# Mixture-of-experts trunk on one core: where the small transposes stand among the expert matrices

## Chip, core and metric

The kernel runs on one core of one Trainium2 chip. The metric is the device time of one execution in microseconds (us), as the median of several runs; lower is better. Everything is float32 at the interface.

## What is computed

One layer of an encoder: attention, a residual layer norm, then a mixture of 32 experts of which each of 1024 tokens takes four, then a second residual layer norm. The change touches the experts only. Cut to that part, the reference is:

```python
def clamped_swiglu(h):
    h_glu = jnp.minimum(h[..., 0::2], SWIGLU_LIMIT)
    h_lin = jnp.clip(h[..., 1::2], -SWIGLU_LIMIT, SWIGLU_LIMIT)
    return h_glu * jax.nn.sigmoid(SWIGLU_ALPHA * h_glu) * (h_lin + 1.0)

def expert_block(args):                 # for each block of rows of one expert
    xblk, e = args
    h = xblk @ w_gate_up[e] + b_gate_up[e]           # 1024 -> 2048
    return clamped_swiglu(h) @ w_down[e] + b_down[e]  # 1024 -> 1024
```

The rows of an expert are gathered by a table, and its results are added back into the token rows with the gate as weight.

## The kernel before

**The expert loop.** The loop `for e in range(NE)` runs over 32 experts in an order that a ranking by load sets. In pass `e` it issues `gate_up(e)`, the gathers of the rows of expert `e + 2` (`gather_x`, `gather_o`), and `down(e - 1)`: the down matrix of one expert is multiplied after the gate and up matrix of the next. An expert's weights come in 1 MB tiles of 128 x 2048 floats: eight for gate and up (k = 0 to 7, called g0 to g7 here; tensors `w10g`, `w11g`, ...), four for down (c = 0 to 3, called d0 to d3; `w10d`, ...). The text writes E11 for the pass e = 11, and so on.

**Three products.** For precision every weight tile is split into a high part `wh` (a cast on ACT, line 607) and a low part `wl` (a subtraction on DVE, line 612), and so are the activations (`xTh`, `xTl`, `aTh`, `aTl`). `mm3` (line 57) issues three matmuls of 128 x 512 for each product; in the trace they read wh with the high activation, wh with the low one, then wl with the high one. So a tile is 4 x 3 = 12 matmuls, and its third is the first that needs `wl`. `wh` and `wl` have three buffers each, and `prep(ci + 3)` splits a tile two ahead of the one that PE multiplies: the cast of a tile can start when PE has finished the tile three before it.

**Two row blocks.** Each expert has 128 main rows. Those for which `ovf(e)` holds have also 32 overflow rows (E1 to E8, then the even ones to E28; 18 in all), computed as four quarters side by side: `go` (32 matmuls after g3 and again after g7 in the trace's count) and `yq` after d3.

**Transposes.** Activations must be transposed by PE into PSUM and copied out. `turn` (line 1133) does one batch: up to four 128 x 128 transposes into the PSUM tile `tp`, of which there is one only (tag `tp`, one buffer), then either `split` (a cast on ACT, line 63, and a subtraction on DVE, line 64) for the main rows, or one ACT copy (line 1138) for the overflow rows. In pass e > 1 there are up to six batches: a(e-1) part 0 and part 1 (the activations of the expert before, four transposes each), ao(e-1) (its overflow activations, two), x(e+1) part 0 and part 1 (the rows of the next expert, four each), xo(e+1) (its overflow rows, two). The dictionaries `between` and `between_d` say after which weight tile each goes: a after g0 and g2, ao after g4, x after g6 and after d0, xo after d2.

**What sets the order.** From E2 on PE's order is the order in which the code is written (`manual_schedule` for PE). The orders on DVE, ACT and POOL come from a scheduler that follows the code where it can. Each engine runs its own instructions in that order.

**The activation function.** `swiglu(...).whole()` runs after g7: on DVE two minima of 128 x 512 from PSUM into `act` (line 1179), two clamps into `lin` (line 1183) and one product over 1024 columns (line 1185); on ACT one Silu between them (line 1180).

**A list on the side.** `list_blocks()` in E1 computes, spread over DVE, a small table that is written to DRAM and read back by two DMAs on ACT's queue: `bt` (line 1117) and `blk` (line 1119), which waits for the first to have landed. They come up in E2.

Of the kernel before, what the change touches and what calls it, by code (L numbers as in the profile page):

```python
# [9 lines left out]
F32 = mybir.dt.float32  # L10
# [10 lines left out]
P = 128  # L21
# [3 lines left out]
KD = D // P  # L25
# [3 lines left out]
NE = 32  # L29
# [16 lines left out]
def trunk_kernel(ctx: ExitStack, tc: tile.TileContext, x, w_qkv, q_norm, k_norm, w_o,  # L46
                 lnm_g, lnm_b, lnf_g, lnf_b, r_w, r_b, w_gu, b_gu, w_dn, b_dn,
                 rope_c, rope_s, out):
    nc = tc.nc
# [12 lines left out]
    def split(hi, lo, src):  # L62
        nc.scalar.copy(hi, src)  # L63
        nc.vector.tensor_tensor(lo, src, hi.bitcast(F32), ALU.subtract)  # L64
# [15 lines left out]
    ident = cp.tile([P, P], F32, name="ident")  # L80
# [93 lines left out]
    with tc.tile_pool(name="p1", bufs=1, side="right", reuse_waits="tile") as p1, \  # L174
# [14 lines left out]
        def load_x(i):  # L189
            xts[i] = p_xq.tile([P, D], F32, tag="rows", name=f"xt{i}")  # L190
            nc.sync.dma_start(xts[i], x[i * P:(i + 1) * P, :])

        def turn_x(i):
            xt = xts[i]
            xT = p_xq.tile([P, 2 * KD, P], F32R, tag="cols", bufs=2, name=f"xT{i}")
            hi, lo = xT[:, 0:KD, :], xT[:, KD:, :]
            for h in range(2):
                tp = ps1.tile([P, 4, P], F32, tag="tp", name=f"tp{i}_{h}")
                for c in range(4):
                    k = 4 * h + c  # L200
                    nc.tensor.transpose(tp[:, c, :], xt[:, k * P:(k + 1) * P], ident)
                split(hi[:, 4 * h:4 * h + 4, :], lo[:, 4 * h:4 * h + 4, :], tp)
            xTs[i] = (hi, lo)
            if i + 1 < NT:
                load_x(i + 1)
            else:
                load_q(0)
# [113 lines left out]
        for i in range(NT):  # L321
# [5 lines left out]
            if 1 < i < NT - 1:  # L327
                turn_x(i + 1)
# [708 lines left out]
    with tc.tile_pool(name="moex", bufs=1, side="right", reuse_waits="tile") as mx, \  # L1037
# [5 lines left out]
        xo, xoT, act, actT, acto, actoT = {}, {}, {}, {}, {}, {}  # L1043
# [77 lines left out]
        def ovf(e):  # L1121
            return 1 <= RANK[e] <= NO
# [10 lines left out]
        def turn(src, hi, lo, nk, nm):  # L1133
            tp = ps_t.tile([P, 4, P], F32, tag="tp", name=f"tp{nm}")
            for c in range(nk):
                nc.tensor.transpose(tp[:, c, :], src[:, c * P:(c + 1) * P], ident)  # L1136
            if lo is None:
                nc.scalar.copy(hi, tp[:, 0:nk, :])
            else:
                split(hi, lo, tp[:, 0:nk, :])  # L1140

        def turn_x(e, part):
            if part == 0:
                xT[e] = [mx.tile([P, KD, P], F32R, tag=f"xT{a}", bufs=2, name=f"xT{a}_{e}") for a in "hl"]
                if ovf(e):
                    xoT[e] = mp.tile([P, 2, P], F32, tag="xoT", bufs=2, name=f"xoT{e}")
            if part == 2 and not ovf(e):
                return
            if part < 2:
                turn(xg[e][:, part * 512:(part + 1) * 512], xT[e][0][:, 4 * part:4 * part + 4, :],  # L1150
                     xT[e][1][:, 4 * part:4 * part + 4, :], 4, f"x{e}_{part}")
            else:
                turn(xo[e], xoT[e], None, 2, f"xo{e}")

        def turn_a(e, part):
            if part == 0:

                tag, bufs = ("xT", 2) if e == NE - 1 else ("aT", 1)
                actT[e] = [mx.tile([P, KD, P], F32R, tag=tag + a, bufs=bufs, name=f"aT{a}_{e}") for a in "hl"]
                if ovf(e):  # L1160
                    actoT[e] = mp.tile([P, 2, P], F32, tag="aoT", bufs=1, name=f"aoT{e}")
            if part == 2 and not ovf(e):
                return
            if part < 2:
                turn(act[e][:, part * 512:(part + 1) * 512], actT[e][0][:, 4 * part:4 * part + 4, :],
                     actT[e][1][:, 4 * part:4 * part + 4, :], 4, f"a{e}_{part}")
            else:
                turn(acto[e], actoT[e], None, 2, f"ao{e}")

        def swiglu(ps, w, nm):  # L1170
            n = len(ps)
# [90 lines left out]
        def down(e, between={}):  # L1262
            y = ys.pop(e, None) or mp.tile([P, D], F32, tag="y", bufs=2, name=f"y{e}")
            yp = ps_g.tile([P, D], F32, tag="gu0", name=f"yp{e}") if e == NE - 1 else \
                ps_y.tile([P, D], F32, tag="y", name=f"yp{e}")
            if ovf(e):
                yq = ps_o.tile([P, 512], F32, tag="o", name=f"yq{e}")
            ah, al = actT[e]
            later = []
            for c in range(KD // 2):  # L1270
                fetch(ci[0] + len(order))
                prep(ci[0] + 3)
                hi, lo, w = wts.pop((e, "d", c))
                for j in range(2):
                    k = 2 * c + j
                    for n in range(2):
                        sl = slice(j * D + n * 512, j * D + (n + 1) * 512)
                        mm3(yp[:, n * 512:(n + 1) * 512], ah[:, k, :], al[:, k, :], hi[:, sl], lo[:, sl],
                            k == 0, k == KD - 1)
                later.append((c, w))  # L1280
                if c == KD // 2 - 1:
                    for cc, w in later if ovf(e) else ():
                        ts = slice(cc * OVF, (cc + 1) * OVF)
                        for j in range(2):
                            for n in range(2):
                                sl = slice(j * D + n * 512, j * D + (n + 1) * 512)
                                m = 2 * j + n
                                mm(yq[m * OVF:(m + 1) * OVF], actoT[e][:, j, ts], w[:, sl],
                                   cc == 0, cc == KD // 2 - 1)
                    later.clear()  # L1290
                ci[0] += 1
                if c in between:
                    between[c]()
            nc.scalar.mul(y, yp, gm_s[:, e:e + 1])  # L1294
            nc.gpsimd.indirect_dma_start(  # L1295
                out=fd, out_offset=bass.IndirectOffsetOnAxis(ap=mi[:, e:e + 1], axis=0),
                in_=y, in_offset=None, bounds_check=T + P - 1, oob_is_err=True, compute_op=ALU.add)
            if e == NE - 1:

                idle = ps_y.tile([P, D], F32, tag="y", name="idle")  # L1300
                for r in range(22):
                    mm(idle[:, 0:512], ah[:, KD - 1, :], hi[:, 0:512])
            if not ovf(e):
                return
            H2 = 2 * OVF
            ya = mp.tile([H2, 512], F32, tag="ya", bufs=1, name=f"ya{e}")
            nc.scalar.mul(ya, yq[H2:P], go_s[H2:P, e:e + 1])
            yo = mp.tile([H2, 512], F32, tag="yo", bufs=2, name=f"yo{e}")
            nc.vector.scalar_tensor_tensor(yo, yq[0:H2], go_s[0:H2, e:e + 1], ya, ALU.mult, ALU.add)
            nc.gpsimd.indirect_dma_start(  # L1310
                out=fd2, out_offset=bass.IndirectOffsetOnAxis(ap=toh[:, e:e + 1], axis=0),
                in_=yo, in_offset=None, bounds_check=2 * (T + P) - 1, oob_is_err=True, compute_op=ALU.add)
# [2 lines left out]
        in_turn = ExitStack()  # L1315
        for e in range(NE):
            between = {}
            between_d = {}
            if e > 0:
                for k, part in zip((0, 2, 4) if e > 1 else range(3), range(3)):  # L1320
                    between[k] = lambda part=part: turn_a(e - 1, part)
            if e + 1 < NE:
                if e == 0:
                    between[X1] = lambda: [turn_x(1, part) for part in range(3)]
                else:
                    for k, part in zip((6, 8, 10) if e > 1 else (3, 4, 5), range(3)):
                        (between if k < KD else between_d)[k % KD] = lambda part=part: turn_x(e + 1, part)
            if e == 0:
                with tc.manual_schedule(engines={mybir.EngineType.DVE}):
                    slots(lambda: prep_lo(2))  # L1330
            gate_up(e, between)
            if e == 1:
                list_blocks()

                in_turn.enter_context(tc.manual_schedule(engines={mybir.EngineType.PE}))
            if e + 2 < NE:
                gather_x(e + 2)
                gather_o(e + 2)
            if e == NE - 1:
                between = {1 + part: lambda part=part: turn_a(NE - 1, part) for part in range(3)}  # L1340
                down(e - 1, between)
            elif e > 0:
                down(e - 1, between_d)
        down(NE - 1)
        in_turn.close()

# [7 lines left out]
    for i in range(NT // 2):  # L1354
        f = slot(order[(len(seq) + 1 + i) % len(order)], f"fs{i}")
# [154 lines left out]
```

## Time and profile before

| | |
|---|---|
| median of 3 runs | 2076.91 us (2074.36 to 2081.57) |
| profiled execution | 2077.01 us, span of the trace 2075.2 us |
| mean granted TensorE clock | 0.991 of full speed |
| PE matmul busy | 2005.0 us (97% of the span) |
| DVE busy | 1599.3 us (77%) |
| ACT busy | 1272.2 us (61%) |
| POOL busy | 540.5 us (26%) |
| DMA | 500.44 MB, mean 241 GB/s |

PE is TensorE's matmuls, PEld its weight loads, which overlap them, DVE is VectorE, ACT is ScalarE, POOL is GpSimd. The end of a matmul is modelled in the trace, so rows are best compared by their starts. A number in brackets at the end of a row is the time for which the engine sat idle before it, with the instruction or engine that released it. "xN" means that N like instructions in a row are shown as one. A cast or split whose input is named `w10d` belongs to the down matrix of expert 10, which is multiplied in pass E11.

### The profile page before, as it was taken

The page shows a single profiled execution, that of the slowest core. Times are in us where ns is not written, and L with a number is a line of the kernel's source. Part 1 is how long each engine was busy: PE and PEld are TensorE (multiplying, and loading weights), DVE is VectorE, ACT ScalarE, POOL GpSimd, SP SyncE. Part 2 cuts the span into 40 slices and gives each one's busy share as a digit, 9 for nine tenths or more (in the row PEclk, how much of TensorE's full clock was granted, in tenths as well). Part 3 has the DMA queues.
Part 4 walks back from the last instruction along what each step waited for, and adds up shares of the span by engine and source line. Part 5 has one row for each costly group of instructions (what it writes and reads, how often), then busy time and mean ns, then how long its engine had stood idle before and what let it go on. Part 6 is the DMA issues. An engine that isn't in the chain of part 4 may idle for free. (4 is left out here: it accounts for less than half of the span.)

```text
span 2075.2 us, 28727 instructions
## 1 busy us (share of the span) xinstructions
PE 2005.0 (97%) x10691; PEld 1425.7 (69%) x10691; DVE 1599.3 (77%) x1649; ACT 1272.2 (61%) x1566; POOL 540.5 (26%) x373
## 2 busy tenths in 40 slices
PE   8998999999997999999999999999999999999997
PEld 6775666665675666666676777767777677677774
DVE  6647778776888787777777877878878787787894
ACT  5655555655554566566566766767667666666674
POOL 0215777776134202212211111011111110111100
PEclk9999999999998999999999999999999999999999
DMA  5216000000645687887788888979889889788875
GB/s 174 72 62 178 31 32 21 30 22 17 226 145 213 257 311 277 304 293 295 279 331 296 355 333 311 374 286 341 338 303 357 319 309 371 283 352 326 335 306 183
DMA packets 106353, 500.44 MB, mean 241 GB/s; under 512 B 16001, under 2 KB 17026, under 8 KB 73442
## 3 DMA queue, kind: packets, MB, share of 16 engines
q1 hardware_dynamic: 87360, 447.02, 55.9%
q0 software_dynamic: 16000, 50.90, 8.7%
q8 instruction: 85, 1.39, 0.3%
q10 hardware_dynamic: 2850, 0.66, 0.2%
q14 instruction: 58, 0.48, 0.1%
HBM read 457.05 MB, written 41.49 MB: 240 GB/s over the span
## 5 line engine op out<-in xcount | busy, mean ns | idle before, releaser
L55 PE MATMUL gu<-wh,xTh 128*128 128x512 f32 x1024 | 419.2, 410 | 1.0 <-ACT xTh L63 1.0
L55 PE MATMUL gu<-wl,xTh 128*128 128x512 f32 x1024 | 401.8, 393 | 0.3 <-DVE wl L612 0.3
L55 PE MATMUL gu<-wh,xTl 128*128 128x512 f32 x1024 | 401.1, 392 | 0.0
L448 POOL TENSOR_TENSOR acc<-acc,pt 128x512 f32<-128x512 f32 x152 | 211.8, 1393 | 79.7 <-ACT pt L444 70.1
L55 PEld LDWEIGHTS gu<-wh,xTh 128*128 128x128 f32 x1024 | 193.1, 189 | 54.7 <-issue 14.2
L55 PEld LDWEIGHTS gu<-wl,xTh 128*128 128x128 f32 x1024 | 192.9, 188 | 43.4 <-DVE wl L612 0.7
L55 PEld LDWEIGHTS gu<-wh,xTl 128*128 128x128 f32 x1024 | 193.7, 189 | 36.9 <-DVE xTl L64 0.2
L55 PE MATMUL yp<-wl,aTh 128*128 128x512 f32 x512 | 201.7, 394 | 9.0 <-DVE wl L612 9.0
L55 PE MATMUL yp<-wh,aTh 128*128 128x512 f32 x512 | 206.0, 402 | 0.0
L598 POOL DMA_INDIRECT xg<-xd,mi x32 | 45.9, 1436 | 609.0 <-PE tpx L1136 599.7
L55 PE MATMUL yp<-wh,aTl 128*128 128x512 f32 x512 | 200.0, 391 | 0.0
L434 DVE TENSOR_REDUCE nm<-sc 128x1 fp32r<-128x1024 f32 x124 | 150.6, 1221 | 51.3 <-PE sc L55 50.4
L444 ACT ACTIVATE pt<-st 128x512 f32<-128x512 f32 x256 | 149.4, 596 | 55.5 <-PE st L55 45.9
L1295 POOL DMA_INDIRECT fd<-y,mi x32 | 78.9, 2467 | 302.4 <-ACT y L1294 302.4
L55 PE MATMUL qkv<-wh,xT 128*128 128x512 f32 x384 | 124.3, 404 | 2.6 <-ACT xT L63 1.4
L55 PEld LDWEIGHTS yp<-wl,aTh 128*128 128x128 f32 x512 | 96.1, 188 | 36.5 <-DVE wl L612 15.3
L55 PE MATMUL po<-pt,vn 128*64 128x256 f32 x1024 | 118.5, 384 | 0.0
L55 PEld LDWEIGHTS yp<-wh,aTh 128*128 128x128 f32 x512 | 96.2, 188 | 31.5 <-issue 14.3
L55 PE MATMUL st<-qs,kT_hi 128*128 128x512 f32 x256 | 112.2, 438 | 3.6 <-ACT pt L444 3.0
L55 PEld LDWEIGHTS yp<-wh,aTl 128*128 128x128 f32 x512 | 96.4, 188 | 18.3
L55 PE MATMUL st<-q,kT_lo 128*128 128x512 f32 x256 | 101.9, 398 | 1.3 <-DVE q L148 1.3
L55 PE MATMUL sc<-kT_hi,qs 128*128 128x512 f32 x256 | 101.4, 401 | 1.0 <-DVE nm L434 0.8
(520 smaller groups left out, 4163.9 us busy)
## 6 DMA issues: line engine op xcount, KB each, us to landing
w0g<-in_expert_w_gate_up SPq DMA_DIRECT2D x8, 1024.0 KB
w1g<-in_expert_w_gate_up SPq DMA_DIRECT2D x8, 1024.0 KB
w2g<-in_expert_w_gate_up SPq DMA_DIRECT2D x8, 1024.0 KB
w3g<-in_expert_w_gate_up SPq DMA_DIRECT2D x8, 1024.0 KB
w4g<-in_expert_w_gate_up SPq DMA_DIRECT2D x8, 1024.0 KB
w5g<-in_expert_w_gate_up SPq DMA_DIRECT2D x8, 1024.0 KB
w6g<-in_expert_w_gate_up SPq DMA_DIRECT2D x8, 1024.0 KB
w7g<-in_expert_w_gate_up SPq DMA_DIRECT2D x8, 1024.0 KB
```

Of the source, the lines that this page charges most:

```text
L55: nc.tensor.matmul(o, lhsT=lhsT, rhs=rhs, start=start, stop=stop)
L434: nc.vector.tensor_reduce(nms[n][:, m:m + 1], sc.pop((n, m)), AX.X, ALU.max, negate=True)
L444: nc.scalar.activation(pts[n, k], st, AF.Exp)
L448: (nc.vector if n == NG - 1 or n == NG - 2 and k > 3 else nc.gpsimd).tensor_tensor(accs[n], pts[n, 0] if k == 1 else accs[n], pts[n, k], A ...
L598: return nc.gpsimd.indirect_dma_start(out=xg[e], out_offset=None, in_=xd, in_offset=bass.IndirectOffsetOnAxis(ap=mi[:, e:e + 1] if rows is ...
L1295: nc.gpsimd.indirect_dma_start(out=fd, out_offset=bass.IndirectOffsetOnAxis(ap=mi[:, e:e + 1], axis=0), in_=y, in_offset=None, bounds_chec ...
```

## The change

From E2 on the batches are placed anew, and the two short ones become one. A new function `turn_o(e)` transposes xo(e+1) into columns 2 and 3 of one `tp` tile and ao(e-1) into columns 0 and 1, and issues two ACT copies from it; it stands after g4. x(e+1) part 0 moves from after g6 to after g5, and part 1 from after d0 to after g7. No batch is left in `down(e - 1)` (except in the last pass, which is as before). a(e-1) stays after g0 and g2. Passes E0 and E1 stay as they were.

```diff
+        def turn_o(e):
+
+            tp = ps_t.tile([P, 4, P], F32, tag="tp", name=f"tpo{e}")
+            if e + 1 < NE and ovf(e + 1):
+                for c in range(2):
+                    nc.tensor.transpose(tp[:, 2 + c, :], xo[e + 1][:, c * P:(c + 1) * P], ident)
+                xoT[e + 1] = mp.tile([P, 2, P], F32, tag="xoT", bufs=2, name=f"xoT{e + 1}")
+                nc.scalar.copy(xoT[e + 1], tp[:, 2:4, :])
+            if ovf(e - 1):
+                for c in range(2):
+                    nc.tensor.transpose(tp[:, c, :], acto[e - 1][:, c * P:(c + 1) * P], ident)
+                nc.scalar.copy(actoT[e - 1], tp[:, 0:2, :])
...
-            between_d = {}
-            if e > 0:
-                for k, part in zip((0, 2, 4) if e > 1 else range(3), range(3)):
-                    between[k] = lambda part=part: turn_a(e - 1, part)
+            if e == 1:
+                for part in range(3):
+                    between[part] = lambda part=part: turn_a(e - 1, part)
+            elif e > 1:
+                between[0] = lambda: turn_a(e - 1, 0)
+                between[2] = lambda: turn_a(e - 1, 1)
+                between[4] = lambda: turn_o(e)
...
-                    for k, part in zip((6, 8, 10) if e > 1 else (3, 4, 5), range(3)):
-                        (between if k < KD else between_d)[k % KD] = lambda part=part: turn_x(e + 1, part)
+                    for k, part in zip((5, 7) if e > 1 else (3, 4, 5), range(3)):
+                        between[k] = lambda part=part: turn_x(e + 1, part)
...
-                down(e - 1, between_d)
+                down(e - 1)
```

What this makes of DVE's order, from the split of d0 to that of d3 in pass E11 (`wl136` to `wl139` are d0 to d3 of expert 10, `xTl_12` the low parts of x(12), `act11` and `lin11` the activation function of expert 11). Before:

```order
L612 TENSOR_TENSOR wl136_10267<-w10d0_10094,wh136_10265 128x2048 [waits DMAHW1_49,PE_49,Activation_49]
L612 TENSOR_TENSOR wl137_10295<-w10d1_10124,wh137_10293 128x2048 [waits DMAHW2_49,PE_49,Activation_49]
L64 TENSOR_TENSOR xTl_12_10282<-tpx12_0_10284,xTh_12_10281 128x512 [waits Activation_49]
L1179 TENSOR_SCALAR act11_10122<-gu11_0_10116 128x512 [waits PE_49]
L1179 TENSOR_SCALAR act11_10122<-gu11_1_10117 128x512 [waits PE_49]
L1183 TENSOR_SCALAR lin11_10123<-gu11_0_10116 128x512
L1183 TENSOR_SCALAR lin11_10123<-gu11_1_10117 128x512
L612 TENSOR_TENSOR wl138_10326<-w10d2_10152,wh138_10324 128x2048 [waits DMAHW3_49,Activation_49]
L1185 SCALAR_TENSOR_TENSOR act11_10122<-lin11_10123,act11_10122 128x1024 [waits DVE_49,Activation_49]
L64 TENSOR_TENSOR xTl_12_10282<-tpx12_1_10340,xTh_12_10281 128x512 [waits Activation_49]
L612 TENSOR_TENSOR wl139_10351<-w10d3_10170,wh139_10349 128x2048 [waits DMAHW4_49]
```

The same stretch on DVE with the change:

```order
L612 TENSOR_TENSOR wl136_10274<-w10d0_10088,wh136_10272 128x2048 [waits DMAHW1_49,PE_49,Activation_49]
L64 TENSOR_TENSOR xTl_12_10262<-tpx12_0_10263,xTh_12_10261 128x512 [waits Activation_49]
L1192 TENSOR_SCALAR act11_10116<-gu11_0_10110 128x512 [waits PE_49]
L612 TENSOR_TENSOR wl137_10292<-w10d1_10118,wh137_10290 128x2048 [waits DMAHW2_49,Activation_49]
L1192 TENSOR_SCALAR act11_10116<-gu11_1_10111 128x512 [waits PE_49]
L64 TENSOR_TENSOR xTl_12_10262<-tpx12_1_10306,xTh_12_10261 128x512 [waits Activation_49]
L1196 TENSOR_SCALAR lin11_10117<-gu11_0_10110 128x512
L1196 TENSOR_SCALAR lin11_10117<-gu11_1_10111 128x512
L612 TENSOR_TENSOR wl138_10330<-w10d2_10146,wh138_10328 128x2048 [waits DMAHW3_49,DVE_49]
L1198 SCALAR_TENSOR_TENSOR act11_10116<-lin11_10117,act11_10116 128x1024 [waits DVE_49,Activation_49]
L612 TENSOR_TENSOR wl139_10348<-w10d3_10164,wh139_10346 128x2048 [waits DMAHW4_49,PE_49,Activation_49]
```

The same eleven instructions stand between the two ends. The first minimum and the first `xTl` now come ahead of the split of d1, and the second `xTl` ahead of the clamps.

ACT's order in pass E2 around the two DMAs of the block list (`wh27` is g7 of expert 2, `wh28` d0 of expert 1). Before:

```order
L1117 DMA bt_85<-ebi_6847 128x2 [waits DVE_49]
L607 CAST wh27_7091<-w2g7_6899 128x2048 [waits DMAHW2_49,PE_49,Activation_49]
L1119 DMA blk_4797<-bt_85 1x256 [waits DMAHW7_49]
L1138 COPY aoT1_6968<-tpao1_7085 128x256 [waits PE_49]
L607 CAST wh28_7109<-w1d0_6917 128x2048 [waits DMAHW3_49,PE_49,Activation_49]
L607 CAST wh29_7137<-w1d1_6948 128x2048 [waits DMAHW4_49,PE_49,Activation_49]
L63 CAST xTh_3_7125<-tpx3_0_7128 128x512 [waits PE_49]
```

ACT's order there with the change:

```order
L1117 DMA bt_85<-ebi_6847 128x2 [waits DVE_49]
L607 CAST wh27_7095<-w2g7_6899 128x2048 [waits DMAHW2_49,PE_49,Activation_49]
L1119 DMA blk_4797<-bt_85 1x256 [waits DMAHW7_49]
L1177 COPY xoT3_7088<-tpo2_7085 128x256 [waits PE_49]
L1181 COPY aoT1_6968<-tpo2_7085 128x256 [waits PE_49]
L607 CAST wh28_7122<-w1d0_6917 128x2048 [waits DMAHW3_49,PE_49,Activation_49]
L63 CAST xTh_3_7111<-tpx3_0_7113 128x512 [waits PE_49]
```

The `blk` DMA still stands ahead of the copy that frees `tp`; a second copy stands behind it, and the cast of x(3) part 0 has moved ahead of one weight cast.

## Rows read from the trace of the kernel before

**Rows 1.** Page, busy us, share and instructions of each engine.

```profile
PE 2005.0 (97%) x10691; PEld 1425.7 (69%) x10691; DVE 1599.3 (77%) x1649; ACT 1272.2 (61%) x1566; POOL 540.5 (26%) x373
```

**Rows 2.** Waits of PE, 900 to 2040 us: releaser, total us, times, longest.

```profile
PE yp L55 <- DVE wl L612: 9.0, 13, 0.9
```

**Rows 3.** Timeline of PE: start, us, instruction, idle before; E11, then E30.

```profile
1184.33 0.38 PE L1136 MATMUL tpxo<-ident,xo 128*128 128x128 f32 x2
...
1184.78 0.40 PE L55 MATMUL yp<-wh,aTl 128*128 128x512 f32 x1
1185.85 0.50 PE L55 MATMUL yp<-wl,aTh 128*128 128x512 f32 x1 [0.68 <-DVE wl L612]
1186.19 0.40 PE L55 MATMUL yp<-wh,aTh 128*128 128x512 f32 x1
...
1981.41 0.50 PE L55 MATMUL yp<-wl,aTh 128*128 128x512 f32 x1 [0.92 <-DVE wl L612]
```

**Rows 4.** Timelines of ACT and DVE in E11, from the tile g5 on.

```profile
1166.74 1.91 ACT L607 CAST wh<-w11g 128x2048 fp32r<-128x2048 f32 x1 [0.80 <-PE gu L55]
1168.55 0.37 ACT L1138 COPY aoT<-tpao 128x256 f32<-128x256 f32 x1
1169.72 1.91 ACT L607 CAST wh<-w10d 128x2048 fp32r<-128x2048 f32 x1 [0.81 <-PE gu L55]
1171.66 2.29 DVE L612 TENSOR_TENSOR wl<-w10d,wh 128x2048 fp32r<-128x2048 f32 x1 [0.69 <-ACT wh L607]
1174.38 2.29 DVE L612 TENSOR_TENSOR wl<-w10d,wh 128x2048 fp32r<-128x2048 f32 x1 [0.42 <-ACT wh L607]
1177.19 1.28 DVE L1179 TENSOR_SCALAR act<-gu 128x512 f32<-128x512 f32 x2
1179.58 2.28 DVE L612 TENSOR_TENSOR wl<-w10d,wh 128x2048 fp32r<-128x2048 f32 x1
1181.78 1.22 DVE L1185 SCALAR_TENSOR_TENSOR act<-lin,act 128x1024 f32<-128x1024 f32 x1
1183.52 2.28 DVE L612 TENSOR_TENSOR wl<-w10d,wh 128x2048 fp32r<-128x2048 f32 x1
```

**Rows 5.** Timeline of PE in E11: matmuls around a batch of two and of four.

```profile
1166.54 0.39 PE L55 MATMUL gu<-wl,xTh 128*128 128x512 f32 x1
...
1167.22 0.39 PE L55 MATMUL gu<-wh,xTl 128*128 128x512 f32 x1
...
1172.24 0.40 PE L55 MATMUL gu<-wl,xTh 128*128 128x512 f32 x1
...
1173.15 0.39 PE L55 MATMUL gu<-wh,xTl 128*128 128x512 f32 x1
```

**Rows 6.** Timeline of PE in E10: overflow matmuls between g7 and d0.

```profile
1136.22 3.64 PE L55 MATMUL go<-w10g,xoT 128*32 128x512 f32 x32
```

**Rows 7.** Timelines of PE and ACT in E2, around the block list's DMA.

```profile
758.60 0.39 PE L55 MATMUL gu<-wl,xTh 128*128 128x512 f32 x1
758.66 0.47 ACTq L1119 DMA_DIRECT2D blk<-bt  x1
759.17 0.37 ACT L1138 COPY aoT<-tpao 128x256 f32<-128x256 f32 x1 [4.12 <-PE gu L55]
759.60 0.66 PE L1136 MATMUL tpx<-ident,xg 128*128 128x128 f32 x4 [0.61 <-ACT aoT L1138]
...
776.06 0.44 PE L1136 MATMUL tpxo<-ident,xo 128*128 128x128 f32 x2 [0.57 <-DVE xTl L64]
```

**Rows 8.** Timeline of PE in E0 and E1: two longer waits and what follows.

```profile
680.32 0.63 PE L1136 MATMUL tpx<-ident,xg 128*128 128x128 f32 x4 [2.34 <-DMA xg<-xd,mi]
...
681.48 0.61 PE L55 MATMUL gu<-wh,xTh 128*128 128x512 f32 x1
...
684.88 0.41 PE L55 MATMUL gu<-wl,xTh 128*128 128x512 f32 x1
...
690.03 0.66 PE L1136 MATMUL tpx<-ident,xg 128*128 128x128 f32 x4 [1.30 <-DVE xTl L64]
```

More of the change, by code (lines that the diff above doesn't have):

```diff
@@ L1144, in turn_x @@
                 xT[e] = [mx.tile([P, KD, P], F32R, tag=f"xT{a}", bufs=2, name=f"xT{a}_{e}") for a in "hl"]
-                if ovf(e):
+                if ovf(e) and e < 3:
                     xoT[e] = mp.tile([P, 2, P], F32, tag="xoT", bufs=2, name=f"xoT{e}")
```

## The prediction

> **What bounds the kernel now.** The page comes first: PE is busy for 97% of the span [rows 1]. The question is then what the remaining idle time of PE is in the expert loop. The waits of PE in that stretch are nearly one line: 9.0 us in 13 waits for DVE's `wl` in down tiles [rows 2]. The timeline shows where: at the third matmul of d3, the first that reads `wl`. Ten waits are alike, one in each odd pass E9 to E27; E29 and E30 have one of 0.94 and 0.92 us, and the last lies in E31, which the change leaves alone; the second and the twelfth are shown [rows 3]. Passes with overflow work after g7 have none, since 3.64 us of `go` matmuls give DVE time [rows 6]. So the loop is bound by PE, except in a stretch of each pass without such work, where DVE is last. There the activation function (two minima, two clamps, one product), two `xTl` and four weight splits stand in one queue.
>
> **Prices.** One matmul step is 0.228 us: from 1167.22 to 1172.24 there are 22 steps [rows 5]; a tile of 12 is 2.74 us. A batch of two costs PE 0.68 - 2 x 0.228 = 0.225 us, a batch of four 0.91 - 0.456 = 0.455 us [rows 5]. That is proportional: joining two batches of two saves nothing (0.00 us). On DVE, start to start: a weight split 2.20 us (1179.58 to 1181.78), a minimum or a clamp 0.60 (1177.19 to 1179.58 holds four), split plus `xTl` 2.81 (1174.38 to 1177.19), so `xTl` 0.60, and the product 1183.52 - 1181.78 - 0.60 = 1.14 [rows 4].
>
> The Trainium skill ("TensorE: Matmul & The Clock Gate", section "Back-to-back issue gap") gives 81 ns for each weight load and matmul of 128 columns in a stream. The trace differs, with 114 ns for a float32 transpose [rows 5]; by the page's price a batch of four would be 0.32 us, and since the number of transposes doesn't change, the sum would be the same.
>
> **Odd passes E9 to E27 (10).** Take T = 1166.54, the last matmul of g4 in E11 [rows 5]. Before, the split of d3 starts at 1183.52, and PE gets on at 1185.85, T + 19.31 [rows 3, 4]. Without the wait it would have been at 1184.78 + 0.228, T + 18.47. PE's work up to there is the same after the change (the xo batch only moves forward), so T + 18.47 stays. Does DVE come sooner? The cast of d0 starts when g5 is done: T + 3.18 before, and T + 3.41 after, since g4 is now followed by four transposes and not two. The split of d0 follows 1.94 us later (1169.72 to 1171.66), at T + 5.35. From there the new order on DVE is: split d0 to 7.55; `xTl` to 8.15; first minimum to 8.75 (its half of g7 is done at about 7.98: g6 ends at 3.41 + 0.455 + 2.74, plus half a tile); split d1 to 10.95 (its cast, begun at 6.61, is done at 8.55); second minimum to 11.55; some 0.20 (an estimate) of waiting for the second `xTl`, whose cast stands on ACT behind the cast of d2 that begins at 9.34 and takes 1.91; `xTl` to 12.35; two clamps to 13.55; split d2 to 15.75; product to 16.89; split d3, 2.28 long, to 19.17, and PE goes on 0.05 later at T + 19.2. So DVE stays last. What the new order gives is the 0.42 us that DVE waited for the cast of d1 [rows 4] and little else; the later start takes 0.225 back. **The wait shrinks by some 0.1 us, not by 0.95** (1184.78 to 1186.19 is 1.41 for two steps). Both `xTl` are still in the stretch: x part 1 moved by one tile, and its `xTl` has only changed places with other work. The xo batch, 0.225 us on PE, stood in the shadow of DVE's delay and now stands where PE is the bound. A short wait at d2 (`wl` at 15.8 against 15.7 when PE wants it) is inside the same time. 10 x 0.11 = -1.1 us.
>
> **E29 and E30 (2).** The same, but no xo batch moves: 0.33 each, -0.7 us.
>
> **Passes with overflow work.** In E10 to E28, even, the wait stays away: DVE's queue is longer by a minimum and a clamp of the overflow rows and, at 0.60 for each, ends with d3 at T + 19.7 (T the last matmul of g4 there), while PE, with 3.64 us of `go` in between [rows 6], wants it at T + 21.7. E3 to E8 are alike. Batches only change places there: 0 us. x part 1 now follows `go` and not a down tile; no row shows that, and I bound it by 0.1 us either way for 17 passes, +-1.8 us, and take 0, since batches after gate and down tiles cost the same.
>
> **The waits that the change adds.** `tp` is one tile, so x part 0 after g5 waits for both copies of `turn_o`. ACT's queue has them behind the cast of g7; the copy started 1.81 us after that cast (1166.74 to 1168.55) [rows 4], two of 0.37 end 2.55 us after it, at T + 2.75, and PE wants `tp` at T + 3.42. Cover 0.67 us, cost 0. Were it gone, x part 0 would wait, and behind it g6, d0's cast and DVE. The gathers on POOL that wait for the freed xo and xg rows start earlier, a pass ahead of their use, and SP's weight loads wait for the same tiles as before: 0.
>
> In **E2** the cover is not there. ACT's queue holds `blk`, which waits for a DMA and ends that wait at 758.66; the copy that frees `tp` followed at 759.17, and PE, which came for it after g6, lost 0.61 us [rows 7]. After the change PE comes after g5, 2.74 - 0.225 = 2.5 us sooner, and the second copy ends 0.37 later: the wait grows by 2.9 us to some 3.5 us. In return the wait of 0.57 us of the xo batch at 776.06 goes [rows 7]; what is late next is PE's own work. Net +2.3 us. And such a pause touches the clock. After a wait of 2.34 us in E0, eight matmul steps from 681.48 to 684.88 took 3.40 us, 0.43 each and not 0.228 (the lower level, 1.2 GHz, for 2.4): 1.6 us lost; after one of 1.30 us the trace shows no such stretch [rows 8]. 3.5 us is beyond the first, so I add +1.6 us.
>
> The Trainium skill ("TensorE: Matmul & The Clock Gate", section "Why this matters for your kernels") also has pauses between matmuls send the clock back to half. It speaks against a new pause, and the trace agrees with its 1.6 us.
>
> **Sum.** -1.1 - 0.7 + 2.3 + 1.6 = +2.1 us on the profiled execution's 2077.0 us: 2079.1. That execution stands 0.1 us above the median of the runs. A measurement of this kernel can tell about 0.3%, 6.2 us, so this is no change.
>
> **Rivals.**
> 1. *No pause in E2*, or one without the slow steps. The DMA's landing decides. For it: `blk` hangs on a transfer, whose time can differ from run to run. Against: ACT's order has not changed around it. Without the slow steps 2077.5; without any wait 2077.0 - 1.8 - 0.6 - 0.6 = 2074.0. Chance 0.14.
> 2. *The stalls go*, as fewer batches among the down tiles would suggest: 10 x 0.95 and 2 x 1.2 (0.25 more, as the recorded waits are), 11.9 us, against 3.9 in E2: 2069.0, faster. For it: DVE has nothing of x in its queue behind d1. Against: the eleven instructions between d0's and d3's splits are the same, and they add up to T + 19.0 even without a gap, against 18.47. Chance 0.05.
> 3. *Slower: the first minimum waits for all of g7.* It now stands ahead of the split of d1. If the wait is met only at the end of g7 (T + 9.34 and not 8.15), DVE stands 1.2 us, of which 0.2 would have been lost later: 0.9 more in ten passes and 0.7 in two, +10 us, with E2 2090.9. It decides from some 0.2 us past its turn. For it: before, both minima came after g7, so no row shows a half finished. Against: in the order the second minimum has a wait of its own on PE, which it would not need. Chance 0.05.
> 4. *Slower: the second copy is late.* Behind d0's cast it would hold PE for 2.2 us in 16 passes, 2114; the order has it ahead. Chance 0.02.
>
> That the batches are not where the change says is excluded on PE, whose order is the written one.
>
> **How the numbers follow.** The forecast has 0.74. Its terms have these bounds: E2 from -1.2 (no wait) to +3.9, the odd passes from 0 to -4 (the 0.33 without the later start), the batch after `go` +-1.8. Most of rival 1 lies inside. Together with some 2 us for medians of few runs, the range is 2073.5 to 2083.5. Faster by over 0.3% is rival 2 (0.05) and a little for what I have missed: 0.06. Slower is rivals 3 and 4: 0.07. The rest, 0.87, is no change.
>
> **What would show it.** Right: in the profile after, the waits of PE for `wl` at d3 are still there, 0.5 to 0.7 us each, twelve of them, with short ones at d2; E2 has a wait of over 3 us before x(3) part 0, released by ACT, and slow steps behind it; no wait of PE before x part 0 in other passes. Wrong: the line of waits for `wl` is gone or under 3 us (rival 2), DVE idles before the first minimum (rival 3), or x part 0 waits for a copy in every pass (rival 4).

## The result, and the profile after

The changed kernel takes **2109.5 us** (median of 4 runs, 2109.3 to 2111.4) where the kernel before takes 2075.6: a ratio of 1.016, 95% interval 1.014 to 1.018. It is 34 us slower. The forecast was 2079.1 us and no change.

The page of the kernel after has a span of 2107.5 us; before it was 2075.2. The line of PE (busy us, share of the span, instructions), against [rows 1]:

```profile
PE 2010.4 (95%) x10691; PEld 1428.2 (68%) x10691; DVE 1600.1 (76%) x1649; ACT 1275.6 (61%) x1566; POOL 549.5 (26%) x373
```

PE does the same 10691 instructions and is busy for 5.4 us more (2010.4 against 2005.0), but the span is 32.3 us longer. So most of the loss is idle time of PE, and the view to open next is that of its waits. Waits of PE after the change (who waited for whom, total us, times, longest); the first line is that of the stretch from 640 to 900 us, the other two of the stretch from 900 to 2080 us:

```profile
PE tpo L1180 <- ACT xoT L1177: 10.2, 3, 6.6
...
PE tpo L1180 <- ACT xoT L1177: 23.6, 13, 1.8
...
PE yp L55 <- DVE wl L612: 4.1, 13, 0.4
```

A wait stands there that the forecast had not named at all: **PE waits for ACT's copy of `xoT`, 16 times, 33.8 us in all.** The old wait for `wl` [rows 2] is down from 9.0 to 4.1 us.

The timeline of PE in E11 shows where it lies: inside the joined batch. (Columns: start, us, instruction, idle time before it and its releaser. The first row is T, the last matmul of g4; the last row is the third step of d3.)

```profile
1181.46 0.39 PE L55 MATMUL gu<-wl,xTh 128*128 128x512 f32 x1
1181.69 0.38 PE L1175 MATMUL tpo<-ident,xo 128*128 128x128 f32 x2
1183.88 0.44 PE L1180 MATMUL tpo<-ident,acto 128*128 128x128 f32 x2 [1.81 <-ACT xoT L1177]
...
1202.69 0.50 PE L55 MATMUL yp<-wl,aTh 128*128 128x512 f32 x1 [0.33 <-DVE wl L612]
```

And ACT beside it:

```profile
1181.66 1.90 ACT L607 CAST wh<-w11g 128x2048 fp32r<-128x2048 f32 x1 [0.80 <-PE gu L55]
1183.46 0.36 ACT L1177 COPY xoT<-tpo 128x256 f32<-128x256 f32 x1
1184.36 0.37 ACT L1181 COPY aoT<-tpo 128x256 f32<-128x256 f32 x1 [0.53 <-PE tpo L1180]
```

`turn_o` is written as: two transposes of xo, the copy of `xoT`, two transposes of acto, the copy of `aoT`. All of it goes through one tile `tp`. ACT reads one half of that tile in its first copy, and the next two transposes write the other half of the same tile; the program makes them wait until the copy is done. The copy in turn stands behind the cast of g7, which ACT had begun 0.03 us before the batch. So PE stands still for the rest of a 1.9 us cast and a 0.36 us copy. The acto transposes start 2.19 us behind the xo transposes; in one stream they follow after 0.22 (shown below). Together with the slower start of the matmul behind them a pass loses **2.02 us**: everything on DVE from d0's split on is late by just that.

The Trainium skill ("PSUM — Partial Sum Buffer", section "PSUM bank collisions raise a hardware error ⚠️") says to guard accumulator memory with semaphores by bank, or by bank and quadrant, and not by address. The wait of 1.81 us is in keeping with that rule: PE waits for a copy that reads only the other half of the tile. What the chip would do without the wait no run here shows.

In E2 the same copy stands behind a DMA issue that waits for another DMA. PE first, then ACT:

```profile
749.13 0.38 PE L1175 MATMUL tpo<-ident,xo 128*128 128x128 f32 x2
756.08 0.69 PE L1180 MATMUL tpo<-ident,acto 128*128 128x128 f32 x2 [6.56 <-ACT xoT L1177]
...
757.42 0.63 PE L55 MATMUL gu<-wl,xTh 128*128 128x512 f32 x1
...
761.26 0.63 PE L55 MATMUL gu<-wl,xTh 128*128 128x512 f32 x1
...
762.55 0.39 PE L55 MATMUL gu<-wh,xTl 128*128 128x512 f32 x1
```

```profile
755.14 0.47 ACTq L1119 DMA_DIRECT2D blk<-bt  x1
755.65 0.37 ACT L1177 COPY xoT<-tpo 128x256 f32<-128x256 f32 x1 [4.61 <-DMA bt<-ebi]
```

PE idles 6.56 us, and behind it the matmul steps are 0.43 us apart (9 steps from 757.42 to 761.26), the lower of the clock's two levels (1.2 GHz; the granted clock from 757.4 to 761.4 us is 0.50), and not 0.228 (2.4 GHz).

**A sum from landmarks.** The start of the first weight split of an expert's tiles on DVE's timeline is a good landmark: E2 is measured from that of expert 2's g0 to that of expert 3's g0, the rest from there to that of expert 31's d0. Before: 730.18, 775.92, 2017.21, so 45.74 and 1241.29 us. After: 726.17, 779.37, 2048.21, so 53.20 and 1268.84. E2 costs 7.5 us more, and the rest 27.6. With 15 waits at 2.02 us, 30.3, the rest has gained 2.7 elsewhere. The head of the program up to expert 2's g0 was 4.0 us shorter in this execution than in that of before; the last section comes back to that.

### The profile page after: what moved, and what is told of

It is laid out like the page before. It is cut to its first block, busy times and chain, and to the rows that moved or that the text cites. A ratio compares the mean times of both kernels' runs of the same rounds, so it can differ in the third digit from the quotient of the medians.

```text
span 2107.5 us, 28721 instructions
## 1 busy us (share of the span) xinstructions
PE 2010.4 (95%) x10691; PEld 1428.2 (68%) x10691; DVE 1600.1 (76%) x1649; ACT 1275.6 (61%) x1566; POOL 549.5 (26%) x373
## 5 line engine op out<-in xcount | busy, mean ns | idle before, releaser
L598 POOL DMA_INDIRECT xg<-xd,mi x32 | 62.1, 1942 | 437.6 <-PE tpx L1136 428.1
```

Of the source, the lines that this page charges most:

```text
L598: return nc.gpsimd.indirect_dma_start(out=xg[e], out_offset=None, in_=xd, in_offset=bass.IndirectOffsetOnAxis(ap=mi[:, e:e + 1] if rows is ...
```

## Experiments

The theory: the loss is the wait inside the joined batch and nothing else. The rival: the new places of the x batches, between gate and up tiles, crowd DVE and ACT there.

**e1_copies_last: the joined batch without the wait.** The kernel after; in `turn_o` the acto transposes come ahead of the first copy:

```
 (two transposes of xo into tp[:, 2:4])
-    xoT[e + 1] = mp.tile(...)
-    nc.scalar.copy(xoT[e + 1], tp[:, 2:4, :])
 (two transposes of acto into tp[:, 0:2])
+    xoT[e + 1] = mp.tile(...)
+    nc.scalar.copy(xoT[e + 1], tp[:, 2:4, :])
     nc.scalar.copy(actoT[e - 1], tp[:, 0:2, :])
```

> The changed kernel with one thing edited: in the joined batch all four transposes run first and both ACT copies after them, so the acto transposes no longer wait for the copy of xoT. Theory (the loss is PE's wait inside the joined batch, 15 times some 2.0 us and some 8 us in E2): the waits of tpo on xoT are gone, the waits of yp on wl at d3 are some 0.5 us each, E2 keeps a pause of PE above 3 us ahead of x part 0 and some slow steps behind it, and the time is some 2078 us, as the forecast had it. Rival (the x batches at g5 and g7 crowd DVE and ACT among the gate and up tiles and that makes the loss): some 2109 us, as before this edit.

Measured: 2078.0 us (11 runs), ratio to before 1.0005, interval 0.9996 to 1.0014. Waits of PE, first from 640 to 900 us, then from 900 to 2080; and its timeline in E11 with T, the four transposes in one stream, and the steps at d2 and d3 that read `wl`:

```profile
PE tpx L1136 <- ACT aoT L1183: 3.9, 1, 3.9
...
PE yp L55 <- DVE wl L612: 4.1, 13, 0.4
```

```profile
1169.83 0.39 PE L55 MATMUL gu<-wl,xTh 128*128 128x512 f32 x1
1170.06 0.38 PE L1175 MATMUL tpo<-ident,xo 128*128 128x128 f32 x2
1170.28 0.38 PE L1178 MATMUL tpo<-ident,acto 128*128 128x128 f32 x2
...
1185.30 0.39 PE L55 MATMUL yp<-wh,aTl 128*128 128x512 f32 x1
1185.70 0.50 PE L55 MATMUL yp<-wl,aTh 128*128 128x512 f32 x1
...
1189.04 0.50 PE L55 MATMUL yp<-wl,aTh 128*128 128x512 f32 x1 [0.33 <-DVE wl L612]
```

The order of six instructions in one function is worth 31.5 us. Nothing else was touched, x parts 0 and 1 still come after g5 and g7: the theory holds, and the rival falls. The landmarks show it pass by pass (from one expert's g0 to the next one's): against the changed kernel each of the 15 passes with the wait is 2.01 to 2.04 us shorter, E2 is 3.9 us shorter, and no other pass differs by more than 0.06 us. That is 34.3 us, more than the 31.5 of the medians; in the traced executions the head of e1 is 4.4 us longer. What is left is the kernel that the forecast had in mind, and its numbers came close: 2078.0 for 2079.1 (by the landmarks +3.5 us in E2 for +3.9, and -2.9 behind it for -1.8), PE goes on at d3 at 1189.04 - 1169.83 = T + 19.21 for T + 19.2, and in E2 a pause of 3.86 us for 3.5. The recorded waits at d3 are 0.33 us and not 0.5 to 0.7, because a part of the delay falls at d2 now: the step at 1185.70 is 0.40 behind the one before it and not 0.228, too little to be listed as a wait.

**e3_join_alone: the join without the moves.** The kernel before with `turn_o` as in the change after g4 from E2 on, x part 0 after g6 and x part 1 after d0 as before (E1 is as in both kernels):

```
-    for k, part in zip((0, 2, 4) if e > 1 else range(3), range(3)):
-        between[k] = lambda part=part: turn_a(e - 1, part)
+    between[0] = lambda: turn_a(e - 1, 0)
+    between[2] = lambda: turn_a(e - 1, 1)
+    between[4] = lambda: turn_o(e)
...
-    for k, part in zip((6, 8, 10) if e > 1 else (3, 4, 5), range(3)):
+    for k, part in zip((6, 8) if e > 1 else (3, 4, 5), range(3)):
```

> The kernel before with the join alone: xo and acto in one batch after g4 by the changed kernel's turn_o (transposes, copy, transposes, copy), x part 0 back after g6 and x part 1 back after d0. Theory: 15 waits of tpo on xoT of some 1.8 us and one of some 6.5 us in E2 with slow steps behind it, some 2110 us. Rival (the moves of the x batches make the loss): some 2076 us.

Measured: 2115.5 us (4 runs), ratio 1.019, interval 1.017 to 1.021. Waits of PE from 900 to 2080 us, and DVE's split of d0 in E11:

```profile
PE tpo L1180 <- ACT xoT L1177: 23.6, 13, 1.8
PE yp L55 <- DVE wl L612: 11.2, 13, 0.9
```

```profile
1193.02 2.29 DVE L612 TENSOR_TENSOR wl<-w10d,wh 128x2048 fp32r<-128x2048 f32 x1 [2.95 <-ACT wh L607]
```

The join alone makes more than the whole loss; the moves soften it. It came 5 us above what I expected, because I had put only the recorded idle time in the sum. T is 1185.65 here, so d0's split starts at T + 7.37; before it was 1171.66 - 1166.54 = T + 5.12. That is 2.25 us a pass: the 2.02, and 0.22 for the xo batch, which before stood in the shadow of DVE's delay at d3 and now stands in front of the chain. By the landmarks behind E2 (782.53 to 2058.55, against 1241.29) the loss is 34.7 us: 24.2 in the ten odd passes E9 to E27 (2.24 to 2.27 each, but 3.87 in E21) and 10.5 in E3 to E7 (2.1 on average; with overflow work after g7 there is no wait at d3 in whose shadow the batch could have stood). E2 (730.26 to 782.53) costs 6.5 more.

**e2_x_moves_alone: the moves without the join.** The kernel before with two numbers changed:

```
-    for k, part in zip((6, 8, 10) if e > 1 else (3, 4, 5), range(3)):
+    for k, part in zip((5, 7, 10) if e > 1 else (3, 4, 5), range(3)):
```

> The kernel before with only the two x batches moved, x part 0 to after g5 and x part 1 to after g7 from E2 on; the batch of acto alone after g4 and the batch of xo alone after d2 as in the kernel before. Theory (the moves themselves are nearly free, the loss is the wait inside the joined batch): no wait of PE on xoT, waits of yp on wl of some 0.6 us, in E2 a pause of some 3.5 us ahead of x part 0 and a few slow steps, some 2078 us where before is 2076.6. Rival (the x batches at g5 and g7 make the loss): 2100 us or more.

Measured: 2076.5 us (10 runs), ratio 0.9995, interval 0.9985 to 1.0004. Waits of PE, from 640 to 900 and from 900 to 2080 us:

```profile
PE tpx L1136 <- ACT aoT L1138: 4.1, 1, 4.1
...
PE yp L55 <- DVE wl L612: 1.0, 3, 0.4
```

The rival is dead: the moves cost only the pause in E2, 3.5 us (729.20 to 778.49, 49.29 for 45.74). Behind E2 they gain 4.6 us by the landmarks (778.49 to 2015.15), and ten of the thirteen recorded waits for `wl` are gone, which I had not expected. The acto batch alone is 0.225 us shorter than the joined one, so d0's split starts at T + 5.13 (1173.77 against T = 1168.64) and the step at d3 at T + 19.00 (1187.64), 0.3 us sooner than before and 0.2 sooner than with the join. What is left of the delay, some 0.5 us behind the T + 18.47 of a PE that never waits, lies in pieces too short to be listed: a wait that is gone from the list is not a delay that is gone.

**e4_e1_E2_as_before and e8_x_moves_E2_as_before: the price of E2.** e1 and e2 with the pass E2 as in the kernel before. The edit of the x batches in e4 is shown; in e4 the batches of a and ao in E2 are put back likewise, and e8 is e2 with `(5, 7, 10) if e > 2 else (6, 8, 10) if e > 1`:

```
-    for k, part in zip((5, 7) if e > 1 else (3, 4, 5), range(3)):
-        between[k] = lambda part=part: turn_x(e + 1, part)
+    for k, part in zip((6, 8, 10) if e == 2 else (5, 7) if e > 2 else (3, 4, 5), range(3)):
+        (between if k < KD else between_d)[k % KD] = lambda part=part: turn_x(e + 1, part)
```

> The kernel of e1_copies_last with the one pass of E2 left as it is in the kernel before. Set against e1_copies_last it gives the price of the joined batch in E2 alone: the forecast's term is 3.9 us (a pause above 3 us and some slow steps), so some 2074 us where e1_copies_last has 2078. The rival, that the pause in E2 costs nothing that the next wait would not have cost, has both equal within 1 us.

> The kernel of e2_x_moves_alone with the pass of E2 left as in the kernel before: x part 0 after g5 and x part 1 after g7 from E3 on, no join. By the landmarks of the traces the moves alone save 5.1 us behind E2 and cost 4.0 us in E2 and E3; with E2 as before the saving stands alone: some 2071.5 us where before is 2076.4, and some 1.5 us below the same moves with the join (e4_e1_E2_as_before, 2072.9). Rival: the saving in e2_x_moves_alone is made only behind the pause in E2 (the loads run ahead there), and the time is that of before.

Measured: e4 2072.9 us (11 runs), ratio 0.9977, interval 0.9960 to 0.9994; e8 2070.7 us (8 runs), ratio 0.9971, interval 0.9961 to 0.9982. By the landmarks E2 takes 46.04 us in e4 (726.00 to 772.04) and 49.26 in e1 (730.61 to 779.87): the pause there costs 3.2 us, in e2 against e8 (49.29 and 46.33) 3.0. The rival of e4, that the pause costs nothing, falls. The medians differ by 5.1 and 5.8; what makes up the rest is not shown. The heads of the profiled executions differ by 4.6 and 1.4 (730.61 against 726.00, 729.20 against 727.85), but there is one trace of each kernel. The saving of the moves is there without the pause in E2, against the rival of e8. As expected the moves alone (e8) are below the moves with the join (e4): the intervals of the two overlap, but behind E2 the landmarks have e8 2.1 us shorter (774.18 to 2010.27, against 772.04 to 2010.24).

**e5_x_g4_g6_o_d0 and e6_e5_product_after_d3: a version meant to beat both.** The join, copies last, put after d0, the x batches one tile earlier (the edit is against e4):

```
-    between[4] = lambda: turn_o(e)
+    between_d[0] = lambda: turn_o(e)
...
-    zip((6, 8, 10) if e == 2 else (5, 7) if e > 2 else (3, 4, 5), range(3))
+    zip((6, 8, 10) if e == 2 else (4, 6) if e > 2 else (3, 4, 5), range(3))
```

> A version meant to beat both: E2 as before; from E3 on x part 0 after g4, x part 1 after g6, and the joined batch of xo and acto, copies last, after d0. Worked out from the chain of DVE: d3's split ends at some 0.5 us behind PE's natural arrival in place of 0.84 us, so 0.34 us less in each of 12 passes: some 2071.5 us. By the rival (x batches among gate and up tiles crowd DVE) it is slower than before, 2080 us or more.

Measured: 2070.7 us (11 runs), ratio 0.9979, interval 0.9970 to 0.9988. It is 0.2% faster than before, and level with e8. The landmarks of the odd passes E9 to E29 are 0.36 to 0.41 us shorter than before, for the 0.34 worked out. What remains is still DVE's queue at d3: T is 1162.13, and the step is at T + 18.92.

```profile
1181.05 0.50 PE L55 MATMUL yp<-wl,aTh 128*128 128x512 f32 x1 [0.31 <-DVE wl L612]
```

To take that too, e6 emits the product of the activation behind d3's split:

```
-    nc.vector.scalar_tensor_tensor(a, lin, 1.0, a, ALU.add, ALU.mult)
+    fin.append(lambda: nc.vector.scalar_tensor_tensor(a, lin, 1.0, a, ALU.add, ALU.mult))
...
 (in down, after a tile's matmuls)
+    if fin:
+        fin.pop()()
```

> The kernel of e5_x_g4_g6_o_d0 with DVE's product of the activation (1.22 us, once a pass) moved from ahead of d3's split to behind it. If the remaining 0.3 us at d3 in each of 13 or 14 passes are due to the length of DVE's queue, as the forecast's chain has it, they go and the time falls by some 4 us to some 2066.5 us. Rival: what the product then delays (the split of the next pass's g0, 1.1 us later) takes the same back, and the time is equal to e5's within 1.5 us or above it.

Measured: 2071.6 us, ratio 0.9982, interval 0.9973 to 0.9991. The experiment failed, since DVE's order in the loop comes from a scheduler and not from the order of the code: the product still stands ahead of d3's split.

```profile
1179.36 1.22 DVE L1201 SCALAR_TENSOR_TENSOR act<-lin,act 128x1024 f32<-128x1024 f32 x1
1180.50 2.28 DVE L612 TENSOR_TENSOR wl<-w10d,wh 128x2048 fp32r<-128x2048 f32 x1
```

By its landmarks it is a second measurement of e5 (behind E2 1236.70 us, 773.92 to 2010.62, against 1236.63, 772.13 to 2008.76), and whether the product could go there was not tried.

**e7_x_g3_g5_o_d0: one tile further.** e5 with `(3, 5)` for `(4, 6)`.

> The kernel of e5_x_g4_g6_o_d0 with the x batches two gate tiles less late: x part 0 after g3, x part 1 after g5. In e5 DVE works without a pause from d1's split (T+8.05) to the end of d3's (T+18.9), xTl of x part 1 among it (0.6 us), and PE waits 0.32 us there. With that part ahead of d1's split the chain is 0.6 us shorter, the waits at d3 go, and the time falls by some 4 us to some 2067 us. Rival: DVE or ACT is late among the gate and up tiles in place of it, and the time is e5's, 2070.7, or above it.

Measured: 2087.8 us (5 runs), ratio 1.005, interval 1.004 to 1.007. Slower: the rival. Waits of PE from 900 to 2080 us, then DVE and PE in E11:

```profile
PE tpx L1136 <- DVE aTl L64: 18.1, 12, 1.5
...
PE yp L55 <- DVE wl L612: 0.7, 2, 0.4
```

```profile
1159.35 2.29 DVE L612 TENSOR_TENSOR wl<-w11g,wh 128x2048 fp32r<-128x2048 f32 x1 [0.42 <-ACT wh L607]
1161.56 0.68 DVE L64 TENSOR_TENSOR aTl<-tpa,aTh 128x512 fp32r<-128x512 f32 x1
```

```profile
1162.30 0.66 PE L1136 MATMUL tpx<-ident,xg 128*128 128x128 f32 x4 [1.51 <-DVE aTl L64]
```

The waits at d3 did go, as I had hoped (4.4 us in e5, 0.7 here). But now one tile of 2.74 us lies between act part 1 (after g2) and x part 0 (after g3), and the reader of `tp` that ends last, `aTl`, stands on DVE behind a weight split. This is the wait of the changed kernel again, on another pair of batches: the next writer of `tp` meets an evictor that queues behind a long operation.

## Why the prediction was wrong

**The step that failed is "The waits that the change adds", with its "Cover 0.67 us, cost 0".** It asked when both copies of `turn_o` leave `tp` free for the *next* batch, x part 0, and found a cover of 0.67 us. It did not ask the same question within the batch, where the acto transposes come right behind the xo transposes with a copy between them: no cover at all. The measured price is 15 x 2.02 us, and 7.5 us in E2 where 3.9 had been put down. [Rows 4] already held what was needed: the copy starts 1.81 us after the cast of g7 and takes 0.37, so it ends 2.18 us after a cast that begins with the batch, and the acto transposes came 2.19 us behind the xo transposes. (That the recorded wait is 1.81 us too is chance: it runs from the end of the xo transposes to the end of the copy.) I read those rows for the batch behind. The order shown ahead of the prediction was DVE's and ACT's; it was PE's own, at the second pair of transposes, that carried the wait. The listed signs of being wrong had the same gap: the line of waits for `wl` stays above 3 us, DVE doesn't idle before the first minimum, x part 0 waits for no copy, and yet the kernel is 34 us slower.

Also, "joining two batches of two saves nothing (0.00 us)" priced the transposes alone. Two batches had two uses of `tp`, many tiles apart; the joined batch has two uses with nothing between them.

**The chain of DVE in odd passes** came true within 0.04 us, shifted by 2.02 us. In E11, T being 1181.46: d0's split at T + 7.36 (forecast 5.35), d3's at T + 18.89 (16.89), PE at T + 21.23 (19.2). From the view of DVE:

```profile
1188.82 2.29 DVE L612 TENSOR_TENSOR wl<-w10d,wh 128x2048 fp32r<-128x2048 f32 x1 [2.94 <-ACT wh L607]
...
1191.66 0.69 DVE L1192 TENSOR_SCALAR act<-gu 128x512 f32<-128x512 f32 x1
1192.27 2.28 DVE L612 TENSOR_TENSOR wl<-w10d,wh 128x2048 fp32r<-128x2048 f32 x1
...
1200.35 2.29 DVE L612 TENSOR_TENSOR wl<-w10d,wh 128x2048 fp32r<-128x2048 f32 x1
```

In e4, which has these moves without the wait and without E2, the terms can be read alone: 3.1 us gained behind E2 (772.04 to 2010.24, against 1241.29), for -1.1 - 0.7 = -1.8 in the sum. The ten odd passes E9 to E27 gain 0.08 to 0.13 us each (forecast 0.11), E29 and E30 0.31 and 0.33 (forecast 0.33). The rest is a tenth in most passes with overflow work and 0.36 in E8, which I had put at 0.

**E2** had the right mechanism: the copy behind `blk`, a pause, slow steps. The price of 3.9 us measured 3.5 in e1 against the kernel before, and 3.2 against e4. In the changed kernel it was 7.5, since PE met the copy a tile earlier, in the middle of the batch after g4.

**The rivals.** 1 (no pause in E2): the pause came. 2 (the stalls go): 4.1 us of listed waits remain after the change. Without the join, in e2 and e8, all but 1.0 us leave the list, but PE still goes on at d3 only 0.3 us sooner than before, not 0.84: most of the delay is cut into pieces and not gone. 3 (the first minimum waits for all of g7): no; the row at 1191.66 above lies ahead of the x part 1 batch, 1192.83, that follows g7. 4 (a copy late behind a cast holds PE 2.2 us in 16 passes, 2114) had the size, the count and the kind, but named the second copy, the cast of d0 and the next batch. The wrong place gave it the wrong chance of 0.02: the order does have the second copy ahead of d0's cast, and that spoke only about the place that I had looked at.

## To carry to other kernels

Where a program's waits go by the whole buffer, as they did here, joining two short batches in one buffer makes each reader of the first part a wait for the writer of the second. Write all parts first, then read: the loss of the change falls here from 34 us to 1.4, which the runs cannot tell from nothing. For every write into a buffer with one copy, ask who read it last, what stands ahead of that reader on its engine, and how much work the writer has in between; within a step as well as between steps. When a change moves instructions, read the waits on the engine that is the bound, not only on the engines around it.

## What the runs showed of the hardware

**A pause and the clock.** PE's wait for a gather in E0 [rows 8] lasted 2.30 to 2.34 us in four of the ten traces, and in those the granted clock fell behind it; in the other six it lasted 1.40 to 1.63 us, and the clock stayed. It also stayed after each of the fifteen waits of 1.81 us in the changed kernel: granted 1.00 over the next 5 us. Busy time by windows, 680 to 685 us, of the kernel before and of the kernel after (columns: window, length, busy us and count for PE, PEld, DVE, ACT and POOL, granted clock, DMA share, GB/s):

```profile
680.00:685.00 5.00, 4.68 (x16) 3.80 (x17) 2.02 (x1) 0.99 (x1) 0.20 (x1) 0.66 1.02 406
```

```profile
680.00:685.00 5.00, 4.74 (x21) 3.31 (x19) 2.68 (x5) 2.22 (x3) 0.00 (x0) 1.00 1.00 395
```

Expert 2's first split starts at 729.2 to 730.6 us in the four (the kernel before, e1, e2, e3) and at 726.0 to 728.0 in the six. Of the 4.0 us between the kernel before and the kernel after, 0.8 are this wait and 1.6 come behind it, where the slow steps are; 1.5 lie before it and were not followed up. The change does not touch the code up to there. Each kernel has one trace, so that the same wait makes runs of one kernel differ is likely but not shown. It is a reason to compare two traces from a landmark on, not from their start.

**What can be told.** e4, e5, e6 and e8 are each 0.2 to 0.3% faster than before, with intervals that exclude no change. That is below the 0.3% that I had called the limit for this kernel; 8 to 11 runs of each did tell it. The landmarks, which leave the head out, agree: from expert 2's g0 to expert 31's d0 the four are 2.8, 4.5, 4.4 and 4.6 us shorter than before.

**Left open.** Whether the two halves of `tp` would bear a write and a read at once was not tried. Why E21 of e3_join_alone costs 1.6 us more than the other odd passes was not followed up.
